# A hybrid decoder layer in seven-product matmuls: the first step on each set of w_out's operands, from eight block products to seven

## The chip, the cores and the metric

The kernel runs on one core of a Trainium2 chip. The metric is the device time of one execution in microseconds (us). An execution has a span, from the first to the last instruction in the profile, and a time, which is a little longer. PE is TensorE, PEld its weight loads, DVE is VectorE, ACT is ScalarE, POOL is GpSimd, SP is SyncE, which here only issues DMAs.

## The reference

A layer over 2048 positions of width 1024: one RMS norm, one input projection to 6144 columns, two token mixers, a norm per head with a gate, one output projection, a residual and a last norm. All is float32.

```python
xn = rms_norm(h, ln_g)
proj = jnp.einsum('bsd,de->bse', xn, w_in)
b_gate, c_gate, x_conv, g_conv, x_lru, g_lru = jnp.split(proj, splits, axis=-1)
y_conv = headwise_rms_norm(short_conv_mixer(b_gate, c_gate, x_conv, conv_w), N_CONV_HEADS, conv_out_g) * silu(g_conv)
y_lru  = headwise_rms_norm(rg_lru_mixer(x_lru, ...), N_LRU_HEADS, lru_out_g) * silu(g_lru)
h = h + jnp.einsum('bse,ed->bsd', concatenate([y_conv, y_lru]), w_out)
return rms_norm(h, final_g)
```

## The kernel before, in words

**Products.** Both projections are cut into 64 steps. A step is a 2x2 block matrix product (stationary blocks S, moving blocks T), done as a Strassen-Winograd scheme with seven products of sums of blocks, numbered 0 to 6. Each operand is split into a high and a low part (`th` and `tl`, or the two halves of a tile `s`), and a product of 128 columns by 512 over four blocks j is 12 matmuls: for each j `s_hi*th`, `s_hi*tl`, `s_lo*th`. Products 0, 1 and 2 add up in one PSUM bank that ACT copies out on the way (`q`, `u`, `rr`); DVE adds the banks and these copies (`combine`).

**Steps.** Steps 0 to 23 and 24 to 47 (kinds l, a, b) are the input projection on the first and second half of the positions; steps 48 to 55 and 56 to 63 (kind o) are the output projection, on the two halves of w_out's rows. Each of these four runs has its own set of 28 pairs of T tiles (7 operands by 4 blocks j). There is room for one set, so a new set replaces the old one tile by tile, at the change from one run to the next. For w_out the set changes between steps 47 and 48 (the first change here) and between steps 55 and 56 (the second).

**Order.** The order on every engine is the order in which the code is written (`manual_schedule`). The loop over steps `n` runs through slots `s`; a slot issues the small work that is due (`tick`), the work of a change of set (`change.slot(q)`), loads or casts for the next step's S tiles (`prep`), and then one product on PE. An ordinary step has seven slots; slot 1 holds product 6 of the step before (`pend`). The last step on an old set has an eighth slot for its own product 6.

**The first step on a set, before.** It does not use the seven sums. It forms the four blocks of the result as eight plain block products in eight slots, on four raw S tiles (`BLOCKS`) and four raw T operands 0, 4, 5 and 7. The step after it runs `late`: its products come in the order `AFTER` = 0, 4, 5, 1, 3, 2, and product 6 in the step after that.

**A change of set, before.** `Change.of_w(q)` is called with q = 0 to 7 in the last old step, 8 to 15 in the first new step and 16 to 21 in the late one. In q = 1 to 8 it cuts 16 raw tiles of w_out (`cut`: an ACT cast for the high part, a DVE subtraction for the low one). `place` loads a sum made earlier from `td` in DRAM into the tile that becomes its low part, at q = 6, 7, 9, 15 for operands 3, 1, 2, 6; these are cut from q = 11 on, operand 6 last, at q = 18 and 19.

**Work prepared ahead.** `jobs` runs in the background of steps 30 to 46. It prepares the S tiles of steps 48, 49, 56 and 57 and stores them to `so`: four raw tiles for the first step on each set (even m), seven for the second (odd m). It also makes the w_out sums and stores them to `td`. The S tiles of later o steps are made from loads of y (`raw<-yd`) and its norms (`zr<-rsd`): DVE multiplies them (`raw<-raw,zr`) and then forms the sums. In steps 56 on, DVE also adds the partial result of the earlier half, loaded from `od` (`ob<-ob,xr`).

**Queues.** All loads are issued by SP in order. DVE and ACT also work in order: an instruction that waits for a load holds up all behind it.

Of the kernel before, what the change touches and what calls it, by code (L numbers as in the profile page):

```python
# [15 lines left out]
ALU = mybir.AluOpType  # L16
# [22 lines left out]
def hymba_kernel(ctx: ExitStack, tc: tile.TileContext, x, xt, w_in, par, lamc, w_gate, w_out, final_g, out):  # L39
# [30 lines left out]
    def aux(name):  # L70
        return small.tile([P, C], F32, tag="aux", bufs=4, name=name)
# [195 lines left out]
    def opens(n):  # L267
        return n > 0 and set_of(n) != set_of(n - 1)


    def load_z(h, m, zr, wait):
        r = [piece("raw") for _ in range(4)]
        fs = []
# [68 lines left out]
    def jobs():  # L342
        tjobs = [(t, j) for t in (2, 3) for j in range(NB)]
        for ph, m in ((0, 0), (0, 1), (1, 2), (1, 3)):
# [5 lines left out]
            for f in fs[2:]:  # L350
                f()
            yield
            if m % 2:
                x_ = aux("s3")
                tt(x_, a11, a21, ALU.subtract)
                tt(a21, a21, a22, ALU.add)
            b = {}

            def blocks():
# [21 lines left out]
            blocks()  # L381
            prev = None
            nothing = lambda: None
            if m % 2:
                items = [(0, a11, lambda: tt(a11, a21, a11, ALU.subtract)), (3, x_, nothing), (2, a21, nothing),
                         (1, a11, nothing), (4, a12, lambda: tt(a12, a12, a11, ALU.subtract)),
                         (6, a22, nothing), (5, a12, nothing)]
            else:
                items = [(n, v, nothing) for n, v in enumerate((a12, a22, a11, a21))]
            for n, (i, v, after) in enumerate(items):  # L390
                if prev:
                    prev()
# [29 lines left out]
    class Change:  # L422
        def __init__(self, t, dst):
            self.t, self.dst, self.r = t, dst, {}
            old = dict(home)
            for i, was in ((5, 0), (4, 1), (0, 3), (7, 2), (3, 4), (1, 5), (2, 6), (6, 2)):
                home[i] = old[was]
            self.order = [(i, j) for i in (5, 4, 0, 7) for j in range(NB)]
            self.loaded = self.split = 0

        def slot(self, q):
# [49 lines left out]
        def of_w(self, q):  # L481
            if q == -3:
                self.load(4)
            if 1 <= q <= 8:
                todo = self.order[self.split:2 * q]
                self.cut(todo)
                self.split += len(todo)
                self.load(min(16, self.split + 6))
            if q in (6, 7, 9, 15):
                self.place((3, 1, 2, 6)[(6, 7, 9, 15).index(q)])  # L490
            self.cut({11: ((3, 0), (3, 1)), 12: ((3, 2), (3, 3)), 13: ((1, 0), (1, 1)), 14: ((1, 2), (1, 3)),
                      15: ((2, 0), (2, 1)), 16: ((2, 2), (2, 3)), 18: ((6, 0), (6, 1)),
                      19: ((6, 2), (6, 3))}.get(q, ()))

        def place(self, i):
            for j in range(NB):
# [3 lines left out]

        def load(self, n):
            for i, j in self.order[self.loaded:n]:
                b = {0: 0, 7: 1, 4: 2, 5: 3}[i]
                self.r[i, j] = piece("traw")
                nc.sync.dma_start(self.r[i, j], w_blocks(self.t, j)[b])
            self.loaded = max(n, self.loaded)
# [503 lines left out]
    def load_next(n, d=2):  # L1010
        if n < N:
            Sn[n] = {}
            kind, h, k = steps[n]
            src = None
            if kind == "o":
                src = so[h, k] if (h, k) in made else None
            elif h == 1 and (k > 0 or kind == "l"):
                src = sd[3 * k + "lab".index(kind)]
            order = {}
            if opens(n):  # L1020
                order = dict(order=BLOCKS, at_=range(4) if kind == "o" else BLOCKS)
            elif opens(n - 1):
                order = dict(order=AFTER, at_=AFTER)
            plan[n] = s_loads(src, Sn[n], **order) if src is not None else s_plan(n, load_s(n, d), Sn[n])

# [6 lines left out]
    with tc.manual_schedule(engines={ENG.PE, ENG.Activation, ENG.DVE, ENG.Pool, ENG.SP}):  # L1032
# [177 lines left out]
        for n in range(PLAIN, N):  # L1210
# [2 lines left out]
            last = n + 1 == N  # L1213
            new = not last and set_of(n + 1) != set_of(n)
            soon = n + 2 < N and set_of(n + 2) != set_of(n + 1)
            put = lru(h, k, 2) if opens(n) and kind == "l" else consumer[kind](h, k)
            if n == 3 * KT + 6:
                work_on[0] = jobs()
            if opens(n):
                cc = {}  # L1220
                for s, (which, i, t) in enumerate(((12, 1, 5), (22, 3, 5), (11, 1, 4), (21, 3, 4),
                                                   (11, 0, 0), (12, 0, 7), (22, 2, 7), (21, 2, 0))):
# [11 lines left out]
                    if s == 4:  # L1234
                        load_next(n + 2, 4)
                continue
            late = opens(n - 1)
            bk = {}
            slots = (0, 6) + ORDER[1:] if not late else AFTER
            for s in range(6 if late else 8 if new or last else 7):  # L1240
# [7 lines left out]
                    change.slot(s - 8)  # L1248
                if new:
                    change.slot(s)  # L1250
                if late:
                    change.slot(16 + s)
                    if s == 0:
                        prep(n, 7)
                elif n > 0 and opens(n - 2):
                    if s == 0:
                        prep(n, 5)
                        prep(n, 6)
                    elif s == 2:
                        prep(n, 7)  # L1260
                elif s == 0:
                    prep(n, 6)
                elif s == 2:
                    prep(n, 7)
                if new and s > 0:
                    if s in (1, 3, 4, 5):
                        prep(n + 1, (1, 3, 4, 5).index(s) + 1)
                    elif s > 5:
                        prep(n + 2, s - 5)
                elif s > 0:  # L1270
                    prep(n + 1, s - 1)
# [87 lines left out]
```

## Time and profile before

| | us |
|---|---|
| median of 3 runs | 1329.51 (1328.81 to 1329.94) |
| the profiled execution, its own time | 1328.63 |
| its span | 1326.9 |
| PE busy | 1295.0 (98%) |
| DVE busy | 1041.1 (78%) |
| ACT busy | 748.7 (56%) |
| granted clock, mean | 0.996 |

PE has 5688 matmuls, 5448 of them on line 993 (`mm`). In a row of the timeline the first number is the start in us from the span's start, the second the duration; `x2` merges two equal instructions; in brackets at the end stand the idle time of the engine before it and what ended that. A duration of a matmul includes its way through the array, so matmuls overlap, and their pitch is shorter than their duration.

### The profile page before, as it was taken

The page shows a single profiled execution, that of the slowest core. Times are in us where ns is not written, and L with a number is a line of the kernel's source. Part 1 is how long each engine was busy: PE and PEld are TensorE (multiplying, and loading weights), DVE is VectorE, ACT ScalarE, POOL GpSimd, SP SyncE. Part 2 cuts the span into 40 slices and gives each one's busy share as a digit, 9 for nine tenths or more (in the row PEclk, how much of TensorE's full clock was granted, in tenths as well). Part 3 has the DMA queues.
Part 4 walks back from the last instruction along what each step waited for, and adds up shares of the span by engine and source line. Part 5 has one row for each costly group of instructions (what it writes and reads, how often), then busy time and mean ns, then how long its engine had stood idle before and what let it go on. Part 6 is the DMA issues. An engine that isn't in the chain of part 4 may idle for free.

```text
span 1326.9 us, 16682 instructions
## 1 busy us (share of the span) xinstructions
PE 1295.0 (98%) x5688; PEld 1059.2 (80%) x5688; DVE 1041.1 (78%) x1251; ACT 748.7 (56%) x1141; POOL 249.6 (19%) x190
## 2 busy tenths in 40 slices
PE   7989999999999999899999999999999999999997
PEld 6867778787878787778888888888888888887886
DVE  7888898999989897979566675667549777659886
ACT  7585758566675657466544545354457433445453
POOL 3204333344334340102010101102011000000000
PEclk9999999999999999999999999999999999999999
DMA  7147777888989888452689999999789987697754
GB/s 291 32 151 246 283 282 249 301 322 284 340 287 325 293 295 302 163 164 97 218 319 298 331 345 337 343 341 366 246 271 323 279 253 250 220 404 286 233 180 160
DMA packets 157958, 355.29 MB, mean 268 GB/s; under 512 B 16944, under 2 KB 51760, under 8 KB 157872
## 3 DMA queue, kind: packets, MB, share of 16 engines
q1 hardware_dynamic: 153264, 338.17, 74.1%
q0 software_dynamic: 4320, 15.73, 3.0%
q8 instruction: 45, 0.74, 0.2%
q14 instruction: 41, 0.34, 0.1%
q10 hardware_dynamic: 288, 0.32, 0.1%
HBM read 217.11 MB, written 137.04 MB: 267 GB/s over the span
## 4 chain that ended last, share of the span: by engine, by line
PE 57%; DVE 21%; DMA 8%; ACT 7%; issue 6%; SPq 1%; POOL 0%; DVEq 0%; ACTq 0%
PE bank L993 54%; DVE s L163 4%; DVE tl L163 2%; DMA s<-so 2%; DVE st L163 2%; PE gate L730 2%; DVE u L704 2%; DVE r L764 2%; ACT i L737 1%; ACT r L737 1%; DVE traw L163 1%; DVE sums L635 1%; DMA raw<-in_w_in_dram 1%; DVE raw L163 1%; DVE u L163 1%
## 5 line engine op out<-in xcount | busy, mean ns | idle before, releaser
L993 PE MATMUL bank<-th,s 128*128 128x512 f32 x3632 | 1132.8, 391 | 13.3 <-ACT q L1293 6.4
L993 PEld LDWEIGHTS bank<-th,s 128*128 128x128 f32 x3632 | 683.1, 188 | 163.1 <-ACT q L1293 7.6
L993 PE MATMUL bank<-tl,s 128*128 128x512 f32 x1816 | 708.6, 390 | 2.3 <-DVE tl L163 2.1
L993 PEld LDWEIGHTS bank<-tl,s 128*128 128x128 f32 x1816 | 341.8, 188 | 75.1 <-DVE tl L163 3.6
L163 POOL TENSOR_TENSOR s<-raw,s 128x512 fp32r<-128x512 f32 x62 | 111.3, 1808 | 248.7 <-ACT s L200 207.9
L200 ACT CAST s<-raw 128x512 fp32r<-128x512 f32 x140 | 85.3, 617 | 78.1 <-PE bank L993 44.4
L163 POOL TENSOR_TENSOR gb<-gb,sg 128x1024 f32<-128x1024 f32 x16 | 43.4, 2712 | 331.0 <-ACT sg L663 292.5
L163 DVE TENSOR_TENSOR s<-raw,s 128x512 fp32r<-128x512 f32 (+1 forms) x125 | 89.4, 738 | 8.6 <-ACT s L1052 4.4
L163 DVE TENSOR_TENSOR s<-s,s 128x512 fp32r<-128x512 f32 x105 | 87.8, 836 | 1.9 <-ACT s L200 1.9
L163 DVE TENSOR_TENSOR tl<-traw,th 128x512 fp32r<-128x512 f32 x85 | 61.0, 750 | 25.1 <-ACT th L438 16.9
L200 ACT CAST s<-s 128x512 fp32r<-128x512 f32 x105 | 64.8, 617 | 13.8 <-DVE s L163 13.8
L704 DVE SCALAR_TENSOR_TENSOR u<-xl,pt,u 128x1024 f32<-128x1024 f32 x48 | 64.4, 1342 | 6.5 <-ACT u L700 5.9
L1293 ACT COPY q<-bank 128x512 f32<-128x512 f32 x58 | 33.9, 584 | 54.4 <-PE bank L993 44.9
L814 DVE SCALAR_TENSOR_TENSOR t<-p,pt,t 128x1024 f32<-128x1024 f32 x32 | 46.5, 1454 | 15.9 <-ACT t L811 15.1
L737 ACT ACTIVATE r<-gate,pt 64x512 f32<-64x512 f32 x64 | 43.7, 683 | 17.3 <-PE gate L730 16.5
L163 DVE TENSOR_TENSOR st<-u,st 64x1024 fp32r<-64x1024 f32 x32 | 49.5, 1547 | 1.2 <-ACT st L715 0.3
L1296 ACT COPY rr<-bank 128x512 f32<-128x512 f32 x31 | 18.1, 584 | 55.5 <-PE bank L993 55.5
L1296 ACT COPY u<-bank 128x512 f32<-128x512 f32 x27 | 15.8, 585 | 54.1 <-PE bank L993 53.9
L163 DVE TENSOR_TENSOR raw<-raw 128x512 f32<-128x512 f32 x41 | 44.9, 1096 | 0.2
L163 DVE TENSOR_TENSOR traw<-traw 128x512 f32<-128x512 f32 x60 | 41.9, 699 | 3.6 <-DMA traw<-in_w_out_dram 2.1
L737 ACT ACTIVATE i<-gate,pt 64x512 f32<-64x512 f32 x64 | 43.7, 683 | 1.1
L163 POOL TENSOR_TENSOR gl<-gl,sg 128x1024 f32<-128x1024 f32 x16 | 40.1, 2508 | 19.0 <-ACT sg L663 19.0
(168 smaller groups left out, 1262.3 us busy)
## 6 DMA issues: line engine op xcount, KB each, us to landing
sd<-s SPq DMA_DIRECT2D x151, 512.0 KB
s<-sd SPq DMA_DIRECT2D x151, 512.0 KB
raw<-in_w_in_dram SPq DMA_DIRECT2D x104, 256.0 KB
raw<-yd SPq DMA_DIRECT2D x64, 256.0 KB
traw<-in_w_out_dram SPq DMA_DIRECT2D x64, 256.0 KB
so<-so SPq DMA_DIRECT2D x22, 512.0 KB
s<-so SPq DMA_DIRECT2D x22, 512.0 KB
yd<-gl SPq DMA_DIRECT2D x32, 256.0 KB
```

Source lines behind the costliest of these rows:

```text
L163: (eng or nc.vector).tensor_tensor(out=out, in0=a, in1=b, op=op)
L200: nc.scalar.copy(dst[i][0], val(i))
L635: nc.vector.tensor_reduce(out=sums[0][:, kt * R:(kt + 1) * R].rearrange("p (q b) -> p q b", q=4), in_=y.rearrange("p (b q a) -> p q b a", ...
L704: nc.vector.scalar_tensor_tensor(out=v["u"], in0=o1[:, 1 + j:1 + j + N2], scalar=lw[j], in1=v["u"], op0=ALU.mult, op1=ALU.add)
L730: nc.tensor.matmul(ps[j], v["gw"][n][:, j, :], v["st"][j][:, sl], start=(n == 0), stop=(n == 1))
L737: nc.scalar.activation(out=g_[hi, sl], in_=v["ps"][j][src], func=AF.Sigmoid, bias=pt[src, bias + k:bias + k + 1])
L764: nc.vector.tensor_tensor_scan(out=r, data0=r, data1=v["u"], initial=init, op0=ALU.mult, op1=ALU.add)
L814: nc.vector.scalar_tensor_tensor(out=tcur["t"], in0=p[:, 2 + j:2 + j + N2], scalar=cw[j], in1=tcur["t"], op0=ALU.mult, op1=ALU.add)
L993: nc.tensor.matmul(bank, a[:, js], b, start=start and n == 0, stop=stop and n == 2, skip_group_check=more)
L1293: nc.scalar.copy(q1, bk["A"])
L1296: nc.scalar.copy(u2, bk["A"])
```

## The change

The first step on each of w_out's two sets takes the same seven products as the other steps, in the order `AFTER`, with product 6 in the following step; the step after it is an ordinary one. Step 24, of kind l, keeps its eight block products (`whole`). W_out's change of set uses slots q = 0 to 14 in place of 0 to 19: three raw operands (12 cuts) at q = 1 to 6, four placed ones, loaded at q = 5 to 8 and cut at q = 8 to 14. `jobs` prepares seven S tiles for steps 48 and 56 too. PE has 24 matmuls less (5664).

```diff
+    def whole(n):
+        return opens(n) and steps[n][0] == "l"
+
+    def late_at(n):
+        return n > 0 and (whole(n - 1) or (opens(n) and not whole(n)))
...
-            if m % 2:
-                items = [(0, a11, lambda: tt(a11, a21, a11, ALU.subtract)), (3, x_, nothing), (2, a21, nothing),
-                         (1, a11, nothing), (4, a12, lambda: tt(a12, a12, a11, ALU.subtract)),
-                         (6, a22, nothing), (5, a12, nothing)]
-            else:
-                items = [(n, v, nothing) for n, v in enumerate((a12, a22, a11, a21))]
+            items = [(0, a11, lambda: tt(a11, a21, a11, ALU.subtract)), (3, x_, nothing), (2, a21, nothing),
+                     (1, a11, nothing), (4, a12, lambda: tt(a12, a12, a11, ALU.subtract)),
+                     (6, a22, nothing), (5, a12, nothing)]
...
-            if 1 <= q <= 8:
+            if 1 <= q <= 6:
                 todo = self.order[self.split:2 * q]
                 self.cut(todo)
                 self.split += len(todo)
-                self.load(min(16, self.split + 6))
-            if q in (6, 7, 9, 15):
-                self.place((3, 1, 2, 6)[(6, 7, 9, 15).index(q)])
-            self.cut({11: ((3, 0), (3, 1)), 12: ((3, 2), (3, 3)), 13: ((1, 0), (1, 1)), 14: ((1, 2), (1, 3)),
-                      15: ((2, 0), (2, 1)), 16: ((2, 2), (2, 3)), 18: ((6, 0), (6, 1)),
-                      19: ((6, 2), (6, 3))}.get(q, ()))
+                self.load(min(12, self.split + 6))
+            if 5 <= q <= 8:
+                self.place((1, 3, 2, 6)[q - 5])
+            self.cut({8: ((1, 0), (1, 1)), 9: ((1, 2), (1, 3)), 10: ((3, 0), (3, 1)), 11: ((3, 2), (3, 3), (2, 0)),
+                      12: ((2, 1), (2, 2), (2, 3)), 13: ((6, 0), (6, 1)), 14: ((6, 2), (6, 3))}.get(q, ()))
...
-            if opens(n):
-                order = dict(order=BLOCKS, at_=range(4) if kind == "o" else BLOCKS)
-            elif opens(n - 1):
+            if whole(n):
+                order = dict(order=BLOCKS, at_=BLOCKS)
+            elif late_at(n):
                 order = dict(order=AFTER, at_=AFTER)
...
-            late = opens(n - 1)
+            late = late_at(n)
...
+                if opens(n - 1) and not late and s == 0:
+                    change.slot(14)
                 if late:
-                    change.slot(16 + s)
+                    change.slot(16 + s if kind != "o" else 8 + s)
```

DVE, at the first change, from the end of step 48 into step 49 (`tl<-tl,th`: the low part of a placed T tile; `sums`, `rt`: norms of the heads; `raw<-raw,zr`: y times its norm for step 50). Before:

```order
L163 TENSOR_TENSOR tl<-tl,th 128x512 x6
L635 TENSOR_REDUCE sums<-t 128x32
L163 TENSOR_TENSOR rt<-sums,rt 128x512
L163 TENSOR_TENSOR tl<-tl,th 128x512 x2
L163 TENSOR_TENSOR raw<-raw,zr 128x512 x2
L163 TENSOR_TENSOR tl<-tl,th 128x512 x2
L163 TENSOR_TENSOR raw<-raw,zr 128x512 x2
```

Now:

```order
L637 TENSOR_REDUCE sums<-r 128x32
L163 TENSOR_TENSOR tl<-tl,th 128x512 x5
L163 TENSOR_TENSOR ob<-bank,rr 128x512 x2
L163 TENSOR_TENSOR raw<-raw,zr 128x512 x2
L163 TENSOR_TENSOR tl<-tl,th 128x512 x2
L637 TENSOR_REDUCE sums<-t 128x32
L163 TENSOR_TENSOR rt<-sums,rt 128x512
L163 TENSOR_TENSOR raw<-raw,zr 128x512 x2
```

The two cuts between the pairs of `raw<-raw,zr` were the last ones of operand 2 and are now the last ones of operand 6; those of operand 6 came four rows later before.

DVE, at the second change, from step 55 into step 57 (`xr<-xr,ob`, `ob<-ob,xr`: adding partial results; `ob<-bank,...`: a product's bank into the result). Before:

```order
L163 TENSOR_TENSOR tl<-tl,th 128x512 x6
L163 TENSOR_TENSOR ob<-ob,xr 128x1024
L163 TENSOR_TENSOR tl<-tl,th 128x512 x4
L163 TENSOR_TENSOR raw<-raw,zr 128x512 x2
L163 TENSOR_TENSOR ob<-ob,xr 128x1024
L163 TENSOR_TENSOR tl<-tl,th 128x512 x2
L163 TENSOR_TENSOR raw<-raw,zr 128x512 x2
```

Now:

```order
L163 TENSOR_TENSOR tl<-tl,th 128x512 x4
L163 TENSOR_TENSOR ob<-bank,q_9994 128x512
L163 TENSOR_TENSOR tl<-tl,th 128x512 x10
L163 TENSOR_TENSOR ob<-bank,rr 128x512 x2
L163 TENSOR_TENSOR raw<-raw,zr 128x512 x2
L163 TENSOR_TENSOR ob<-ob,xr 128x1024
L163 TENSOR_TENSOR tl<-tl,th 128x512 x2
```

Fourteen cuts of placed operands now stand ahead of the first `raw<-raw,zr`; the last two, of operand 6, stand behind it and behind the first `ob<-ob,xr`.

SP, at the second change, up to the load for that first `ob<-ob,xr` (`s<-so_124`, `s<-so_125`: S tiles of steps 56 and 57; `fg`: the last gain; `tl<-td_130` to `td_133`: a placed operand; `xr<-od_138`). Before:

```order
L868 DMA fg<-in_final_g_dram 128x1024
L226 DMA s<-so_125 128x1024
L499 DMA tl<-td_130 128x512
L499 DMA tl<-td_131 128x512
L499 DMA tl<-td_132 128x512
L499 DMA tl<-td_133 128x512
L226 DMA s<-so_125 128x1024
L873 DMA xr<-od_138 128x1024
L226 DMA s<-so_125 128x1024
L294 DMA raw<-yd_86 128x512 x2
```

Now:

```order
L870 DMA fg<-in_final_g_dram 128x1024
L501 DMA tl<-td_130 128x512
L501 DMA tl<-td_131 128x512
L501 DMA tl<-td_132 128x512
L501 DMA tl<-td_133 128x512
L226 DMA s<-so_124 128x1024
L226 DMA s<-so_125 128x1024 x2
L300 DMA raw<-yd_86 128x512 x2
L290 DMA zr<-rsd_89 128x1024
L300 DMA raw<-yd_86 128x512 x2
L290 DMA zr<-rsd_89 128x1024
L875 DMA xr<-od_138 128x1024
```

Ahead of `xr<-od_138` now stand all four loads of y with their norms, and the fourth placed operand (before, the fourth came behind both `xr` loads).

More of the change, by code (lines that the diff above doesn't have):

```diff
@@ L352, in jobs @@
             yield
-            if m % 2:
-                x_ = aux("s3")
-                tt(x_, a11, a21, ALU.subtract)
-                tt(a21, a21, a22, ALU.add)
+            x_ = aux("s3")
+            tt(x_, a11, a21, ALU.subtract)
+            tt(a21, a21, a22, ALU.add)
             b = {}
@@ L383, in jobs @@
             nothing = lambda: None
-            if m % 2:
-                items = [(0, a11, lambda: tt(a11, a21, a11, ALU.subtract)), (3, x_, nothing), (2, a21, nothing),
-                         (1, a11, nothing), (4, a12, lambda: tt(a12, a12, a11, ALU.subtract)),
-                         (6, a22, nothing), (5, a12, nothing)]
-            else:
-                items = [(n, v, nothing) for n, v in enumerate((a12, a22, a11, a21))]
+            items = [(0, a11, lambda: tt(a11, a21, a11, ALU.subtract)), (3, x_, nothing), (2, a21, nothing),
+                     (1, a11, nothing), (4, a12, lambda: tt(a12, a12, a11, ALU.subtract)),
+                     (6, a22, nothing), (5, a12, nothing)]
             for n, (i, v, after) in enumerate(items):
@@ L425, in __init__ @@
             old = dict(home)
-            for i, was in ((5, 0), (4, 1), (0, 3), (7, 2), (3, 4), (1, 5), (2, 6), (6, 2)):
+            for i, was in (((5, 0), (4, 1), (0, 3), (7, 2), (3, 4), (1, 5), (2, 6), (6, 2)) if t == 1 else
+                           ((0, 0), (4, 1), (5, 3), (1, 2), (3, 4), (2, 5), (6, 6))):
                 home[i] = old[was]
-            self.order = [(i, j) for i in (5, 4, 0, 7) for j in range(NB)]
+            self.order = [(i, j) for i in (0, 4, 5) for j in range(NB)]
             self.loaded = self.split = 0
@@ L502, in load @@
             for i, j in self.order[self.loaded:n]:
-                b = {0: 0, 7: 1, 4: 2, 5: 3}[i]
+                b = {0: 0, 4: 2, 5: 3}[i]
                 self.r[i, j] = piece("traw")
@@ L1215, in hymba_kernel @@
             soon = n + 2 < N and set_of(n + 2) != set_of(n + 1)
-            put = lru(h, k, 2) if opens(n) and kind == "l" else consumer[kind](h, k)
+            put = lru(h, k, 2) if whole(n) else consumer[kind](h, k)
             if n == 3 * KT + 6:
                 work_on[0] = jobs()
-            if opens(n):
+            if whole(n):
                 cc = {}
@@ L1250, in hymba_kernel @@
                     change.slot(s)
+                if opens(n - 1) and not late and s == 0:
+                    change.slot(14)
                 if late:
-                    change.slot(16 + s)
+                    change.slot(16 + s if kind != "o" else 8 + s)
                     if s == 0:
                         prep(n, 7)
-                elif n > 0 and opens(n - 2):
+                elif late_at(n - 1):
                     if s == 0:
@@ L1264, in hymba_kernel @@
                     prep(n, 7)
-                if new and s > 0:
+                if new and s > 0 and whole(n + 1):
                     if s in (1, 3, 4, 5):
```

## The prediction, made before the changed kernel ran

> **What bounds the kernel now.** I read the page's busy times first, then the chain that ended last, PE's waits, and tables by stretches of 10 us around the two places where w_out's set changes.
>
> ```profile
> span 1326.9 us, 16682 instructions
> PE 1295.0 (98%) x5688; PEld 1059.2 (80%) x5688; DVE 1041.1 (78%) x1251; ACT 748.7 (56%) x1141; POOL 249.6 (19%) x190
> PE 57%; DVE 21%; DMA 8%; ACT 7%; issue 6%; SPq 1%; POOL 0%; DVEq 0%; ACTq 0%
> ```
>
> PE is the bound of nearly the whole span, so matmuls taken away there are worth their pitch, as long as nothing else is late. Whether something is shows in the stretches (columns: PE, PEld, DVE, ACT and POOL busy, granted clock, DMA share, GB/s):
>
> ```profile
> 1010.00:1020.00 10.00, 10.00 (x46) 8.29 (x45) 8.37 (x7) 4.26 (x7) 3.28 (x1) 1.00 1.06 381
> 1020.00:1030.00 10.00, 10.00 (x46) 8.29 (x45) 9.13 (x13) 7.69 (x14) 1.27 (x2) 1.00 1.01 283
> ...
> 1150.00:1160.00 10.00, 10.00 (x46) 8.29 (x45) 6.44 (x11) 4.50 (x10) 0.00 (x0) 1.00 1.01 361
> 1160.00:1170.00 10.00, 10.00 (x46) 8.29 (x45) 7.96 (x11) 4.74 (x9) 1.07 (x2) 1.00 1.04 408
> 1170.00:1180.00 10.00, 10.00 (x46) 8.29 (x45) 1.43 (x3) 3.10 (x6) 0.00 (x0) 1.00 1.04 402
> 1180.00:1190.00 10.00, 10.00 (x46) 8.29 (x45) 4.93 (x7) 5.22 (x11) 0.00 (x0) 1.00 1.04 403
> 1190.00:1200.00 10.00, 9.14 (x41) 7.25 (x40) 9.15 (x14) 5.15 (x10) 0.53 (x1) 1.00 1.04 398
> 1200.00:1210.00 10.00, 8.92 (x40) 7.04 (x39) 9.96 (x17) 5.16 (x10) 0.53 (x1) 1.00 0.82 300
> ```
>
> At both changes PE runs without a gap while the DMA engines are full (share 1.01 and more) for tens of us; DVE is nearly full too at the first. At the second, 400 GB/s seems to be all that the transfers get. PE is covered there only by how early things were asked for, and the change asks for them later against PE.
>
> **What the change takes away.** The eight block products of an old first step show in ACT's copies of their banks, one per product from the fifth on. First row: the sixth product of step 48; the others: the sixth to eighth of step 56.
>
> ```profile
> 1022.20 0.59 ACT L793 COPY ob<-bank 128x512 f32<-128x512 f32 x1 [0.82 <-PE bank L993]
> ...
> 1178.52 0.59 ACT L793 COPY ob<-bank 128x512 f32<-128x512 f32 x1 [1.04 <-PE bank L993]
> 1181.24 0.59 ACT L793 COPY ob<-bank 128x512 f32<-128x512 f32 x1 [1.09 <-PE bank L993]
> 1183.96 0.59 ACT L793 COPY ob<-bank 128x512 f32<-128x512 f32 x1 [1.09 <-PE bank L993]
> ```
>
> They are 2.72 us apart: one product, 12 matmuls, 0.227 us each. Two products fewer are worth 5.44 us. A copy starts some 0.2 us behind its product, so step 48 goes from 1005.7 to 1027.4, and step 56 from 1162.0 to 1183.8. With six products in these steps, the next ones would begin at 1022.0 and 1178.3, and product 6 of the first step (in slot 1 of the next) at 1024.7 and 1181.0. PE's waits near here, which may go or stay:
>
> ```profile
> PE bank L993 <- ACT rr L1296: 0.5, 1, 0.5
> ...
> 1198.38 0.50 PE L993 MATMUL bank<-th,s 128*128 128x512 f32 x1 [0.86 <-ACT rr L1296]
> 1205.20 0.50 PE L993 MATMUL bank<-th,s 128*128 128x512 f32 x1 [1.08 <-DVE ob L163]
> ```
>
> The first is the only wait of PE from 990 to 1060. Each comes of ACT or DVE being behind in the step after the first; if PE is held up before, they have caught up, so I count all three as gone: -0.45 and -1.94.
>
> **First change, DVE's queue.** Product 6 now needs its low parts a step earlier. The cuts of its blocks 2 and 3 stand behind the first pair of `raw<-raw,zr`, and that pair waits for a load:
>
> ```profile
> 1011.07 3.28 POOL L163 TENSOR_TENSOR gb<-gb,sg 128x1024 f32<-128x1024 f32 x1 [35.67 <-ACT sg L663]
> ...
> 1008.01 1.29 DVE L163 TENSOR_TENSOR tl<-traw,th 128x512 fp32r<-128x512 f32 x2
> 1009.22 0.68 DVE L163 TENSOR_TENSOR gb<-bank,rr 128x512 f32<-128x512 f32 x1
> 1009.82 2.34 DVE L764 TENSOR_TENSOR_SCAN r<-r,hl,u 128x1024 f32<-128x1024 f32 x1
> 1012.08 3.42 DVE L163 TENSOR_TENSOR tl<-traw,th 128x512 fp32r<-128x512 f32 x2
> 1015.42 1.27 DVE L645 SCALAR_TENSOR_TENSOR gl<-r,pt,gl 128x1024 f32<-128x1024 f32 x1
> ...
> 1020.74 1.25 DVE L635 TRANSPOSE_TENSOR_REDUCE sums<-r 128x32 f32<-128x1024 f32 x1
> 1021.90 3.68 DVE L163 TENSOR_TENSOR tl<-tl,th 128x512 fp32r<-128x512 f32 x6
> ...
> 1029.51 1.29 DVE L163 TENSOR_TENSOR raw<-raw,zr 128x512 f32<-128x512 f32 x2 [0.22 <-DMA zr<-rsd]
> 1030.73 1.29 DVE L163 TENSOR_TENSOR tl<-tl,th 128x512 fp32r<-128x512 f32 x2
> ```
>
> Six cuts take 3.68, a pitch of 0.60; the pair at 1012.08 took 2.13 more than two others (1.29), while POOL's multiplication `gb<-gb,sg` (first row) ran beside it. The scan now has the two cuts of 1008.01 less ahead of it, 1.2, so it starts at 1008.6. From there DVE has the scan (2.3), 14 cuts (8.4), POOL's hold (2.1), two `f1` of 1.2, one reduction (1.2) and three bank additions of 0.7 (2.1): it comes to the `raw` pair at 1027.1. The last cut of operand 2, for the sixth product, is done two cuts and two bank additions earlier (2.5), at 1024.6; PE has two matmuls left then and ends step 48 at 1025.1, 3.1 late. Then the pair waits for `zr`. On SP the bytes from the twelfth raw tile of w_out, the last in both orders, up to that `zr` are the same: four raw tiles fewer (1.05 MB), one placed operand more (1.05 MB), eight S tiles in both. The queue is full, so I keep 1029.5. The cut of block 2 is done at 1029.51 + 1.22 + 0.69 = 1031.4, and five matmuls later (1.1) the next product begins at 1032.5, where a PE without stalls would begin it at 1027.4: 5.1 us lost (it contains the 3.1). Net: -2.72 + 5.1 - 0.45 = **+1.9**. Low end, if `zr` is there when DVE comes: 3.1 lost, -0.1. High end, with a further us from S tiles of step 49, asked for behind the y loads: +2.9.
>
> **Second change, SP's queue.** DVE has time here, but the same two cuts stand behind `raw<-raw,zr` and `ob<-ob,xr`:
>
> ```profile
> 1175.12 0.32 SPq L873 DMA_DIRECT2D xr<-od  x1
> 1182.96 0.32 SPq L873 DMA_DIRECT2D xr<-od  x1
> ...
> 1182.99 1.23 DVE L163 TENSOR_TENSOR ob<-ob,xr 128x1024 f32<-128x1024 f32 x1 [4.69 <-DMA xr<-od]
> 1184.13 2.49 DVE L163 TENSOR_TENSOR tl<-tl,th 128x512 fp32r<-128x512 f32 x4
> 1186.94 1.29 DVE L163 TENSOR_TENSOR raw<-raw,zr 128x512 f32<-128x512 f32 x2 [0.32 <-DMA zr<-rsd]
> 1190.78 1.22 DVE L163 TENSOR_TENSOR ob<-ob,xr 128x1024 f32<-128x1024 f32 x1 [2.54 <-DMA xr<-od]
> ```
>
> The placed operands 1, 3 and 2, asked for from slots 5 to 7 of the old step on (1154), wait on SP for the old product that reads their tiles, with S tiles queued behind them; at 7.8 us from issue to use they are there by 1174, and PE needs the last of them at 1177. Not so operand 6. DVE waited for both `xr`, and each landed 7.8 us behind its issue. Ahead of the first `xr` SP now has 1.05 MB for the fourth placed operand, one S tile (0.52) and the four y loads with two norms (2.10) more, and four raw tiles (1.05) less: +2.62 MB. At the 402 GB/s of these stretches it lands 6.5 us later, at 1189.5. The S tile that step 57 opens with has the bytes ahead that the first `xr` had, without the last half MB: 1.3 us before 1183.0, so PE waits at 1178.3 until 1181.7, does product 0 and seven matmuls of product 6 (to 1186.0), and waits again for the cut at 1189.5 + 1.14 + 0.69 = 1191.3. The next product begins at 1192.4 instead of 1183.8: 8.7 lost. Net: -2.72 + 8.7 - 1.94 = **+4.0**. Low end: if the queue, not full before 1160 (the stretch 1150 to 1160 moved 361), takes half of the added bytes for nothing, 5.4 lost, +0.7. High end, at 361 GB/s: 7.3 for 6.5, +4.8.
>
> **The clock.** A gap of 5.3 us at PE has a price of its own:
>
> ```profile
> 97.21 0.79 PE L993 MATMUL bank<-th,s 128*128 128x512 f32 x1 [3.06 <-ACT q L1293]
> ...
> 97.00:100.20 3.20, 2.99 (x7) 2.41 (x8) 3.17 (x4) 3.17 (x5) 0.00 (x0) 0.50 0.72 258
> ```
>
> Behind a gap of 3.06 the granted clock was 0.50, and PE did 7 matmuls in 3.2 us instead of 14: 1.6 us. Behind the gaps of 1.08 and less above, it stayed at 1.00. I take **+1.5**; ends 0 and +1.7.
> The Trainium skill, TensorE: Matmul & The Clock Gate, section "Part 1: The HAM clock gate", says that the clock halves only after a whole idle window of some 3.4 us, and that the window runs freely. By that rule a gap of 5.3 may or may not hold a whole window, and the sum without a drop is 1.5 lower; the gap of 3.06 here was shorter than such a window and the clock fell all the same.
>
> **The rest.** Per set, four cuts fall away on ACT and DVE (in the sum above) and an ACT copy becomes DVE additions (in it too). The two jobs each make three more S tiles: three casts, three subtractions and four sums of a tile, three stores of 0.52 MB, in steps 30 to 43, and every later part of the jobs moves by some slots. PE there has one gap in 400 us:
>
> ```profile
> L993 PE MATMUL bank<-th,s 128*128 128x512 f32 x1135 | 352.3, 389 | 0.6 <-DMA s<-sd 0.6
> ```
>
> DVE's and ACT's part is covered by PE's products; if that cover fails, a bank copy is late next. I take 0; ends -0.6 (this gap goes) and +1 (another like it, since the y loads now follow other stores).
>
> **Sum.** 1.9 + 4.0 + 1.5 = +7.4 on the profiled execution's 1328.63: 1336.0. The median of the runs is 0.9 above that execution, well inside the range, so I leave it at 1336.0. Ends: +0.0 - 0.1 + 0.7 - 0.6, so about 1328.6, and 2.9 + 4.8 + 1.7 + 1 = +10.4, 1339.0; I take 1328.5 to 1340.
>
> **Rivals.**
> *The loads are in time, and it is faster.* PE's 5.44 and the old waits are then saved: 1328.63 - 5.44 - 2.39 = 1320.8; with the first change as forecast, 1325.4. It decides at the first `xr`: landed before 1180.8 (1182.6, when PE needs the cut, less 1.8 of DVE), 8.7 earlier than I expect. For it: SP is ahead of PE by four raw tiles at 1154. Against: 2.6 MB more at 400 GB/s.
> *Short waits.* Both changes at their low ends and no drop of the clock: +0.6 to +3, 1329 to 1332, no change that can be told. For it: DMA had 361 GB/s before 1160 and may have had room.
> *The clock stays full*, by the skill's window or because the wait is split in two: 1334.5. Slower all the same.
> *More stalls.* The S tiles of step 57, asked for behind the two `xr`, land late too: over 1340. Against: they land 1 to 4 us behind the first `xr`, and PE is 8.7 later.
> That the change doesn't remove the products can't be: PE's order has 24 matmuls less.
>
> **Chances.** Forecast with the clock's drop 0.43, without it 0.20, more stalls 0.05: slower 0.68. Short waits 0.20. In time 0.12. By over 0.2% is 2.7 us, about what a measurement here can tell from no change: faster 0.12, same 0.20, slower 0.68.
>
> **What would show it.** PE's waits should have a new one of some 5 us near 1186, with a cut `tl` by name, DVE behind `xr<-od`; one of 2 to 3 near 1024 to 1030 before a `tl`, DVE behind `zr<-rsd`; a granted clock of 0.50 for 3 us behind the first. The prediction is wrong if the first `xr` lands before 1185 or PE has no gap before a `tl` in these places.

## The result, and the profile after

| | before | after |
|---|---|---|
| median of the runs (us) | 1329.94 (5 runs, 1328.81 to 1330.55) | 1343.55 (5 runs, 1340.8 to 1345.6) |
| the profiled execution, its own time | 1328.63 | 1345.6 |
| its span | 1326.9 | 1343.8 |

After over before is 1.0105, with a 95% interval of 1.0093 to 1.0116: 13.6 us slower by the medians, 16.9 between the two profiled executions (that of the changed kernel is the slowest of its five runs). The direction was as forecast, the size was not: 1336.0 was forecast, 1340 was the upper end.

From the page of the changed kernel, its span, its busy times and the chain that ended last:

```profile
span 1343.8 us, 16674 instructions
PE 1295.1 (96%) x5664; PEld 1057.3 (79%) x5664; DVE 1049.0 (78%) x1263; ACT 748.5 (56%) x1139; POOL 248.7 (19%) x190
PE 53%; DVE 20%; DMA 13%; issue 6%; ACT 5%; SPq 2%; POOL 0%; DVEq 0%; ACTq 0%; POOLq 0%
```

PE has 24 matmuls less and is as long busy as before, mostly since some of them ran at half the clock. In the chain PE went from 57% to 53%, DMA from 8% to 13%. What PE waited for in the whole span (us in total, times, longest):

```profile
PE bank L995 <- DVE tl L163: 9.6, 8, 3.7
...
PE bank L995 <- DMA s<-sd: 5.8, 1, 5.8
PE bank L995 <- DMA s<-so: 4.6, 3, 3.5
```

Before, the row with `tl` had 2.1 us, that with `s<-sd` 0.6, and there was no wait for `s<-so`. The 5.8 us of `s<-sd` are one wait, and it stands far from both changes of set, as the three long gaps on PE's timeline show:

```profile
752.04 0.80 PE L995 MATMUL bank<-th,s 128*128 128x512 f32 x1 [5.82 <-DMA s<-sd]
...
1193.33 0.80 PE L995 MATMUL bank<-th,s 128*128 128x512 f32 x1 [3.47 <-DMA s<-so]
...
1203.09 0.57 PE L995 MATMUL bank<-tl,s 128*128 128x512 f32 x1 [3.66 <-DVE tl L163]
```

The first is the start of step 35, in the stretch where `jobs` prepares work; the others are products 0 and 6 in step 57. The same columns by stretches of 10 us as in the prediction:

```profile
740.00:750.00 10.00, 6.22 (x28) 4.80 (x26) 6.55 (x9) 4.87 (x7) 1.43 (x1) 0.97 1.07 243
750.00:760.00 10.00, 7.96 (x26) 6.42 (x27) 1.96 (x4) 1.10 (x2) 0.00 (x0) 0.69 1.03 404
1020.00:1030.00 10.00, 9.01 (x38) 6.45 (x36) 10.00 (x12) 7.38 (x14) 2.48 (x1) 1.00 1.05 391
1030.00:1040.00 10.00, 7.04 (x30) 5.48 (x31) 7.57 (x13) 3.16 (x5) 0.73 (x1) 1.00 1.06 216
1190.00:1200.00 10.00, 6.10 (x19) 4.59 (x19) 3.23 (x6) 2.13 (x5) 0.00 (x0) 0.83 1.04 405
1200.00:1210.00 10.00, 6.91 (x23) 5.54 (x24) 8.65 (x13) 3.17 (x7) 0.00 (x0) 0.83 1.03 405
```

PE has holes at step 35, at the first change (1020 to 1040) and at the second (1190 to 1210), each with the DMA engines full, and the granted clock falls behind the first and the last.

Where the time went can be told for the two profiled executions, because PE's order of matmuls is known: take the start of a step in each trace, after minus before. The difference grows by 7.9 us from step 34 to step 48 (the jobs), by 2.8 from 48 to 50 (the first change), by 6.1 from 56 to 59 (the second), and by 0.2 elsewhere: 16.9 in sum. These three numbers are used for every kernel below.

**The jobs.** In both kernels the y loads of the second job take SP some 9 us. Before, SP issues four td stores, and then these loads at slot 4 of step 33; four S tiles follow, for the steps being computed:

```profile
715.04 1.80 SPq L378 DMA_DIRECT2D td<-traw  x4
...
719.48 0.67 SPq L294 DMA_DIRECT2D raw<-yd  x1
...
726.76 1.69 SPq L287 DMA_DIRECT2D zr<-rsd  x2
728.55 2.83 SPq L226 DMA_DIRECT2D s<-sd  x4
```

After, the first job has seven tiles, so the same things come five slots later, at slots 1 and 2 of step 34:

```profile
726.66 0.43 SPq L678 DMA_DIRECT2D bd<-in_w_gate_dram  x1
732.09 2.18 SPq L383 DMA_DIRECT2D td<-traw  x4
...
735.52 0.82 SPq L300 DMA_DIRECT2D raw<-yd  x1
...
742.53 1.65 SPq L293 DMA_DIRECT2D zr<-rsd  x2
744.36 5.07 SPq L226 DMA_DIRECT2D s<-sd  x7
```

SP stands from 727.1 to 732.1 before the td stores, whose sums DVE has not yet made, and only then issues the y loads. Seven S tiles have piled up behind them. One is for product 0 of step 35, which is asked for five slots ahead of its use, where the others have six. It is used at 752.04. The stop there and the slow clock behind it, less the old wait of 0.6, make 7.1 of the 7.9; nearly all of the rest is one stop of 0.4 in step 43, where PE waited for a copy of ACT, and no other kernel's profile has that stop.

**First change.** DVE from the scan to the last cuts of operand 6:

```profile
1016.69 2.34 DVE L766 TENSOR_TENSOR_SCAN r<-r,hl,u 128x1024 f32<-128x1024 f32 x1
1018.95 1.27 DVE L163 TENSOR_TENSOR tl<-tl,th 128x512 fp32r<-128x512 f32 x2
1020.14 3.43 DVE L647 SCALAR_TENSOR_TENSOR gl<-r,pt,gl 128x1024 f32<-128x1024 f32 x1
...
1030.66 3.05 DVE L163 TENSOR_TENSOR tl<-tl,th 128x512 fp32r<-128x512 f32 x5
1034.15 1.29 DVE L163 TENSOR_TENSOR ob<-bank,rr 128x512 f32<-128x512 f32 x2 [0.44 <-ACT rr L1303]
1037.44 1.29 DVE L163 TENSOR_TENSOR raw<-raw,zr 128x512 f32<-128x512 f32 x2 [1.99 <-DMA zr<-rsd]
1038.65 1.29 DVE L163 TENSOR_TENSOR tl<-tl,th 128x512 fp32r<-128x512 f32 x2
```

This is the forecast order: DVE behind, POOL's hold (2.2 us, now on `gl`), then the pair that waits for `zr` ahead of the cuts.

**Second change.** The first `xr` on SP's timeline:

```profile
1193.35 0.32 SPq L875 DMA_DIRECT2D xr<-od  x1
```

And on DVE's, what waits for it and for `zr` of the same queue:

```profile
1197.30 1.29 DVE L163 TENSOR_TENSOR raw<-raw,zr 128x512 f32<-128x512 f32 x2 [5.36 <-DMA zr<-rsd]
...
1201.21 1.23 DVE L163 TENSOR_TENSOR ob<-ob,xr 128x1024 f32<-128x1024 f32 x1 [2.62 <-DMA xr<-od]
1202.35 1.29 DVE L163 TENSOR_TENSOR tl<-tl,th 128x512 fp32r<-128x512 f32 x2
```

It landed 7.9 us behind its issue, and the cuts came after it.

### The profile page after: what moved, and what is told of

It reads as the page before. It is cut to its first block, busy times and chain, and to the rows that moved or that the text cites. A ratio compares the mean times of both kernels' runs of the same rounds, so it can differ in the third digit from the quotient of the medians.

```text
span 1343.8 us, 16674 instructions
## 1 busy us (share of the span) xinstructions
PE 1295.1 (96%) x5664; PEld 1057.3 (79%) x5664; DVE 1049.0 (78%) x1263; ACT 748.5 (56%) x1139; POOL 248.7 (19%) x190
## 4 chain that ended last, share of the span: by engine, by line
PE 53%; DVE 20%; DMA 13%; issue 6%; ACT 5%; SPq 2%; POOL 0%; DVEq 0%; ACTq 0%; POOLq 0%
PE bank L995 51%; DVE s L163 5%; DMA s<-so 2%; DVE u L706 2%; DVE tl L163 2%; DMA tl<-td 2%; DVE st L163 2%; PE gate L732 2%; DVE traw L163 1%; DVE sums L637 1%; DMA raw<-in_w_in_dram 1%; DMA xcol<-in_xt_dram 1%; DMA s<-sd 1%; DVE r L766 1%; DMA sd<-s 1%
## 5 line engine op out<-in xcount | busy, mean ns | idle before, releaser
L163 DVE TENSOR_TENSOR tl<-traw,th 128x512 fp32r<-128x512 f32 x77 | 53.7, 729 | 25.2 <-ACT th L441 13.4
L739 ACT ACTIVATE r<-gate,pt 64x512 f32<-64x512 f32 x64 | 43.8, 684 | 16.9 <-PE gate L732 16.1
L163 DVE TENSOR_TENSOR raw<-raw,zr 128x512 f32<-128x512 f32 x64 | 41.3, 686 | 12.4 <-DMA zr<-rsd 12.3
L163 DVE TENSOR_TENSOR raw<-raw 128x512 f32<-128x512 f32 x47 | 49.1, 1044 | 0.4
```

The lines of the kernel that those rows point to most:

```text
L163: (eng or nc.vector).tensor_tensor(out=out, in0=a, in1=b, op=op)
L739: nc.scalar.activation(out=g_[hi, sl], in_=v["ps"][j][src], func=AF.Sigmoid, bias=pt[src, bias + k:bias + k + 1])
```

## The experiments

Theory A: the three costs are separate and each is one of order: the y loads of the jobs ahead of an S tile that has little slack; DVE's backlog and the cuts behind `zr`; the bytes ahead of `xr` on SP. Theory B: the three more S tiles per job (three stores of 0.52 MB each) cost time wherever they stand. The other rivals are given with each run. Time is the median, the ratio is to the kernel before on the same chip with its 95% interval. The kernels ran on several chips, so two kernels are best compared by their ratios. The last three columns come from one profiled execution of each: how much the difference of PE's step starts to those of before grows over these steps (us).

| kernel | time | ratio | 34 to 48 | 48 to 50 | 56 to 59 |
|---|---|---|---|---|---|
| after | 1343.55 | 1.0105 [1.0093, 1.0116] | 7.9 | 2.8 | 6.1 |
| jobs_shift | 1336.81 | 1.0058 [1.0042, 1.0074] | -0.9 | 2.9 | 6.2 |
| jobs_alone | 1337.35 | 1.0065 [1.0047, 1.0083] | 7.4 | 0.1 | -0.2 |
| second_only | 1334.36 | 1.0044 [1.0027, 1.0062] | -0.7 | 0.2 | 6.4 |
| first_only | 1339.75 | 1.0081 [1.0066, 1.0096] | 8.2 | 1.2 | 0.3 |
| cut_ahead | 1339.5 | 1.0068 [1.0053, 1.0083] | 7.4 | 2.1 | 0.8 |
| bytes_early | 1342.4 | 1.0087 [1.007, 1.0104] | 7.7 | 1.3 | 3.4 |
| clock_fill | 1342.31 | 1.0091 [1.0077, 1.0105] | 4.6 | 2.2 | 6.9 |
| best | 1328.07 | 0.998 [0.9969, 0.9991] | -0.9 | 1.6 | -3.8 |
| td_pool | 1339.9 | 1.0082 [1.0065, 1.0098] | 3.4 | 2.1 | 7.2 |
| dve_relief | 1328.22 | 0.9995 [0.9986, 1.0004] | -0.9 | 4.2 | -3.7 |
| best2 | 1327.7 | 0.9983 [0.9975, 0.9992] | -0.9 | -0.7 | 0.7 |
| best3 | 1324.17 | 0.9963 [0.9949, 0.9977] | -0.9 | -0.3 | -3.9 |

### The jobs: jobs_shift, jobs_alone, td_pool

**jobs_shift**, the changed kernel with a pause behind the first job:

```diff
-            yield from (None,) * 2
+            yield from (None,) * (4 if (ph, m) == (0, 0) else 2)
```

> The changed kernel with two more slots of pause behind the first job, so that the y loads of the second job are issued in step 34, slot 4, as before the change, and no longer in slot 2 behind the td stores; the later jobs move by one slot at most. Theory A (the place of these loads on SP: the S tile for product 0 of step 35 stands behind them): PE's 5.8 us gap at the start of step 35 is under 1 us, the clock there stays at 1.00, and the time falls by about 7, to 1335 to 1338. Theory B (the three more S tiles per job, 1.57 MB of stores each, cost time wherever they stand): 1342 to 1345, with the gap somewhere else in steps 34 to 37.

PE has no wait at all in 690 to 800, and the time is within theory A's range: 7.7 above the kernel before instead of 13.6. SP still stands before the td stores, but three S tiles now go ahead of the y loads:

```profile
733.26 1.78 SPq L383 DMA_DIRECT2D td<-traw  x4
...
737.74 1.44 SPq L226 DMA_DIRECT2D s<-sd  x3
739.22 0.42 SPq L300 DMA_DIRECT2D raw<-yd  x1
```

The same instructions and bytes, two slots later: theory B falls.

**jobs_alone**, the kernel before with seven tiles in the even jobs, three of them used by nothing:

```diff
-                items = [(n, v, nothing) for n, v in enumerate((a12, a22, a11, a21))]
+                items = [(0, a12, nothing), (1, a22, nothing), (2, a11, nothing),
+                         (3, a21, lambda: tt(a21, a21, a22, ALU.add)),
+                         (4, x_, lambda: tt(a11, a21, a11, ALU.subtract)),
+                         (5, a21, lambda: tt(a12, a12, a11, ALU.subtract)), (6, a12, nothing)]
```

> The kernel before, where the first and the third job also make seven S tiles (three of them, and four sums, are not used by anything), with the slots of the changed kernel; nothing is changed where the sets change. Theory A: 8 us slower than before, some 1337.5, with a gap of 5 to 6 us at the start of step 35 and the clock at 0.50 behind it. Rival: the jobs cost so much only together with the changed steps 48 and 56: 1329 to 1331.

8.2 slower, with one long wait, in step 35:

```profile
PE bank L996 <- DMA s<-sd: 6.4, 1, 6.4
```

So the largest cost of the change is there without any change at steps 48 and 56.

**td_pool**, the changed kernel with the td stores on POOL's queue:

```diff
-                    at(1, lambda: [nc.sync.dma_start(to[n], v) for n, v in enumerate((b22, b11, b12, b21))])
+                    at(1, lambda: [nc.gpsimd.dma_start(to[n], v) for n, v in enumerate((b22, b11, b12, b21))])
```

> The changed kernel with the stores of the w_out sums to td issued by POOL instead of SP; the y loads keep their place in step 34, slot 2. Theory A1 (half of the jobs' cost is SP standing 5.3 us before the td stores until DVE has the sums, with the y loads and the S tiles behind them): the S tile of step 35 comes 5 us earlier, PE's gap there falls from 5.8 to about 1, the clock stays, and the time falls by 6 to 7, to 1336 to 1338. Theory A2 (the 9 us of y loads ahead of that S tile are enough by themselves): a gap of 4 to 5.8 us stays, 1341 to 1344.

Neither: the gap at the start of step 35 fell to 2.4, as PE's timeline shows.

```profile
748.60 0.50 PE L995 MATMUL bank<-th,s 128*128 128x512 f32 x1 [2.37 <-DMA s<-sd]
```

The granted clock (third number from the end in the table by stretches) fell all the same, for 3.4 us instead of 6.8.

```profile
750.00:753.00 3.00, 3.00 (x9) 2.35 (x8) 0.00 (x0) 0.00 (x0) 0.00 (x0) 0.50 1.03 410
```

Step 35 lost 4.3 instead of 8.1. SP's stand before the td stores is worth 3.8 of it; the y loads ahead of the S tile, the rest. How much of that rest comes of the y loads' new slot, and how much of the tile being asked for a slot later than the others, was not taken apart.

### One change at a time: second_only, first_only

In **second_only** step 48 keeps its eight block products and its old change of set, in **first_only** step 56:

```diff
     def whole(n):
-        return opens(n) and steps[n][0] == "l"
+        return opens(n) and (steps[n][0] == "l" or set_of(n) in OLD)
+
+    OLD = (2,)
```

(`OLD = (3,)` in first_only; with it go the raw tiles of that job, and the old operands, places and slots in that `Change`)

> Only step 56 takes seven products; step 48 keeps its eight block products, so the first job makes four tiles and the y loads of the second job stay in step 33, slot 4. Theory A: +6 from the second change, +0.7 from the last job's place: 1335 to 1337. Theory B (tiles cost time wherever they stand, half of 8 for one job): 1338 to 1341.

> Only step 48 takes seven products; step 56 keeps its eight. Theory A: +7.3 from the first job's shift of the y loads, +2.8 from the first change: 1338 to 1341, with the gap at the start of step 35. Theory B (half of 8 for one job, +2.8): 1335 to 1337.

Both are clearly outside theory B, and the costs stand where theory A has them. Second_only, 5.2 slower, is 0.6 below theory A's range: all its cost stands at steps 56 to 58, and the 0.7 expected for the last job's place did not come. First_only is 10.6 slower, of which 8.2 stand in the jobs. The first change itself came out between 1.2 and 2.9 in six executions that have it as changed (after, jobs_shift, first_only, bytes_early, clock_fill, td_pool; median 2.2).

### The cuts, the bytes, the clock: cut_ahead, bytes_early, clock_fill

**cut_ahead**, the changed kernel with the last cuts of operand 6 ahead of the slot's due work:

```diff
+                if opens(n - 1) and not late and s == 0:
+                    change.slot(14)
                 tick()
...
-                if opens(n - 1) and not late and s == 0:
-                    change.slot(14)
```

> The changed kernel with the cuts of operand 6, blocks 2 and 3, written ahead of the slot's other work in steps 49 and 57, so that on DVE they stand before the pair of multiplications by zr (and, in step 57, before the addition of xr). Theory A (these cuts are late for their place in DVE's queue alone): PE's waits of 1.6 us in step 49 and of 3.7 us in step 57 go, and with the latter one of the two clock drops (1.7 us): 7.0 less, 1335.5 to 1338. The 3.5 us wait for the S tile of step 57 stays. Rival (their own loads from td are late too, or the banks' additions are the next to be late): 2 to 4 less, 1339.5 to 1341.5, with a wait of 1 to 3 us left in step 57 or 58.

The time, 1339.5, is at the edge of the rival's range and not in theory A's. At the second change alone it is as theory A has it, 5.3 less: of PE's waits in 1140 to 1240 the one for the cuts is gone.

```profile
PE bank L995 <- DMA s<-so: 3.9, 2, 3.5
```

At the first change it is not told apart from the spread of the others (2.1 against 1.2 to 2.9): the wait for the cuts went, and one for an S tile of step 49 came instead, here of 2.0.

```profile
PE bank L995 <- DVE tl L163: 2.4, 3, 1.6
PE bank L995 <- DMA s<-so: 2.0, 1, 2.0
```

**bytes_early**, the changed kernel with `fg` loaded in step 52, and the xr loads of step 55 four slots earlier:

```diff
-        if ph == 1 and m == 2:
+        if ph == 0 and m == 4:
             fg[0] = wt("t", "fg")
...
-            at(5, lambda: load(0))
-            at(6, lambda: load(1))
+            at(1 if (ph, m) == (0, 7) else 5, lambda: load(0))
+            at(2 if (ph, m) == (0, 7) else 6, lambda: load(1))
```

> The changed kernel with 1.57 MB taken out of SP's crowded stretch before step 57: the broadcast load of fg moves from step 56 to step 52, the two xr loads of step 55 from its slots 4 and 5 to 0 and 1. Theory A (the S tile that opens step 57 is late by the bytes ahead of it: 1.57 MB at 404 GB/s is 3.9 us): the 3.5 us wait at the start of step 57 goes with its clock drop (1.7): 5.2 less, 1337 to 1339.5; the wait before the cuts of operand 6 stays at 3 to 4 us, since PE and xr are earlier by the same. Rival (SP's issue, held up by buffers, sets it): within 1.5 of the changed kernel, 1342 to 1345.

The wait for the S tile at the start of step 57 is gone, so the bytes were its cause. But only 2.7 were won at this change, and the time, 1342.4, is in the rival's range, though not for the rival's reason: the wait for the cuts grew.

```profile
1198.71 0.80 PE L995 MATMUL bank<-tl,s 128*128 128x512 f32 x1 [5.16 <-DVE tl L163]
```

PE came there 5.4 earlier (a wait of 3.47, its restart, and the slow clock behind it), the landing of `xr` that fixes the cut only the 3.9 of its bytes: 3.66 + 1.5 = 5.16. My expectation had both move alike.

**clock_fill**, the changed kernel with transposes in PE's waits, whose results are not used:

```diff
+                if (n, s) == (35, 0):
+                    for _ in range(40):
+                        nc.tensor.transpose(bk[b][:, 0:P], ident, ident)
+                if (n, s) == (57, 0):
+                    spun[0] = None
+                    spin(24)
...
                         for j in range(NB):
+                            if (n, j) == (57, 2):
+                                spin(24)
                             mm(B, S6, T, 6, j, alone and j == 0, j == NB - 1, not alone)
```

> The changed kernel with PE kept at work in its three long waits by 128x128 transposes whose results are not used: 40 ahead of product 0 of step 35, 24 ahead of product 0 of step 57, 24 between blocks 1 and 2 of product 6 in step 57. The waits themselves stay. Theory A (each drop of the granted clock to 0.50 costs half its length: 3.4, 1.7 and 1.7 us): 6.8 less, 1335.5 to 1338, with the clock at 1.00 through steps 35 and 57. Rival (PE would only reach its next wait sooner, or transposes don't count for the clock): 1341 to 1346.

The time is in the rival's range, and in steps 56 to 58 for its first reason. In step 35 the clock stayed at 1.00 and 2.5 us were won, not 3.4: of the 6.8 us at half clock PE had worked only in the last 4.2 (752.0 to 756.2), which cost some 2; the S tile also came 0.5 earlier against PE's steps. At step 57 nothing was won.

```profile
1186.20 2.78 PE L531 MATMUL spin<-ident 128*128 128x128 f32 x24
1189.86 0.50 PE L995 MATMUL bank<-th,s 128*128 128x512 f32 x1 [0.87 <-DMA s<-so]
...
1194.10 2.78 PE L531 MATMUL spin<-ident 128*128 128x128 f32 x24
1200.53 0.78 PE L995 MATMUL bank<-tl,s 128*128 128x512 f32 x1 [3.41 <-DVE tl L163]
```

The first drop was avoided, but PE then only stood longer before the cuts, whose time `xr` sets; and the rest of that wait, 3.41, still brought a drop. Td_pool shows the same without any transposes: there the clock stayed at 1.00 behind the first wait of step 57 (3.47, as in the changed kernel), and the second was 5.39 instead of 3.66.

### Taking the costs away: best, dve_relief, best2, best3

**best** is the changed kernel with the edits of jobs_shift, cut_ahead and bytes_early.

> The changed kernel with three edits together: two more slots of pause behind the first job, the cuts of operand 6 ahead in steps 49 and 57, and fg and the xr loads of step 55 earlier. Theory A: the added costs go one by one, -7.3 for the jobs, -1.6 at the first change, -7 to -10 at the second: 1324.5 to 1328, that is 1 to 4 below the kernel before, of the 5.4 that two products are worth; what is left is DVE's backlog at the first change (2 to 3 us). Rival (the second change is bound by its transfers as a whole): a wait of 3 us or more in step 57, 1329 to 1333.

1328.07, at the upper end of theory A's range and 0.2% below the kernel before. The second change is now worth 3.8, the jobs 0.9 (the old wait of 0.6 in step 34 is gone); the first still costs 1.6.

**dve_relief** takes 2.2 us of DVE's time out of the first change:

```diff
-        at(d0 + 3, lambda: head_sums(h, kt, y))
+        at(d0 + (4 if h and kt == 2 * KT - 1 else 3), lambda: head_sums(h, kt, y))
...
-        at(4 + late, lambda: tt(g, g, sg[0], ALU.mult, nc.gpsimd))
+        at(4 + late, lambda: tt(g, g, sg[0], ALU.mult, eng or nc.gpsimd))
...
-                silu(g)
+                silu(g, 0, nc.vector if h and k == KT - 1 else None)
```

> The kernel with the three edits, and 2.2 us taken out of DVE's queue ahead of the last cuts of operand 2 at the first change: the multiplication gb by sg of step 47 runs on DVE (1.2 us) instead of POOL, beside which a DVE instruction took 2.2 longer, and the reduction of r (1.25 us) comes one slot later. Theory A (what is left of the first change's cost is DVE's backlog): PE's waits for cuts in step 48, 1.6 and 0.6 us, go, and the time falls by 1.5 to 2.2, to about 1326. Rival (step 49 waits for an S tile from so in any case): that wait of 1.5 us grows by what was won, and the gain is under 0.7, 1327.4 to 1328.5.

The time is in the rival's range, and by the profile the first change now costs 4.2, where it cost 1.6 in best. Step 48 was 2.2 shorter, but the S tile of step 49 came when it came: PE's wait for it grew from 1.5 to 3.7, and the clock was at 0.50 for 6.8 us behind it.

```profile
1034.26 0.80 PE L995 MATMUL bank<-th,s 128*128 128x512 f32 x1 [3.70 <-DMA s<-so]
```

**best2** also moves the y loads behind those S tiles:

```diff
-                if s == 3:
-                    load_next(n + 2, 3 if late else 4)
+                if s == (5 if late and kind == "o" else 3):
+                    load_next(n + 2, 1 if late and kind == "o" else 3 if late else 4)
```

> The same with the y loads of steps 50 and 58 issued two slots later (slot 5 of steps 48 and 56), behind the S tiles of slots 4 and 5. Theory A (S tiles and cuts are all that PE waits for there): the S wait in step 49 goes too, 3 to 3.7 below the kernel with three edits, 1324 to 1325.5. Rival (zr then comes later, and DVE's additions of the banks stand behind raw by zr): a new wait of PE for a bank in step 49, 50, 57 or 58, and 1326 to 1329.

The time, 1327.7, is in the rival's range; by the profile both theories hold, one at each change. The first is now 0.7 better than before. At the second `zr` comes later, DVE's `ob<-ob,xr` stands behind it, ACT's square of `ob` behind that, and the copy that frees PE's bank behind ACT's square:

```profile
1191.93 0.50 PE L995 MATMUL bank<-th,s 128*128 128x512 f32 x1 [2.89 <-ACT rr L1300]
```

**best3** moves the y loads of step 50 alone:

```diff
-                if s == (5 if late and kind == "o" else 3):
-                    load_next(n + 2, 1 if late and kind == "o" else 3 if late else 4)
+                if s == (5 if n == 48 else 3):
+                    load_next(n + 2, 1 if n == 48 else 3 if late else 4)
```

> The kernel with the three edits and the relief of DVE, where the y loads of step 50 alone come two slots later (slot 5 of step 48); those of step 58 stay in slot 3 of step 56. Theory A (each change is bound by what PE waits for there, and the two do not touch each other): the first change costs as little as with both loads moved (-0.7 over steps 48 and 49 instead of +1.6), the second as little as with three edits (-3.8 over steps 56 to 58), with no wait of PE over 1.2 us in either: a span of 1321 to 1323, 4 to 6 below the profiled execution of the kernel before, and a time of 1324 to 1326. Rival (the gain at the first change is lost again before step 56): 1327 to 1328.5.

4.8 below the kernel before, as theory A has it (-0.3 instead of -0.7 at the first change). PE's waits that are left, first in 1000 to 1080, then in 1140 to 1240:

```profile
PE bank L995 <- ACT rr L1300: 1.0, 1, 1.0
PE bank L995 <- DVE tl L163: 0.7, 1, 0.7
PE bank L995 <- DMA s<-so: 0.3, 1, 0.3
...
PE bank L995 <- DMA s<-so: 0.8, 2, 0.6
```

These 4.8 are not the two products alone. In the stretches of the table the stops of the kernel before that are gone were worth 4.1 (the waits of 0.59, 0.45, 0.86 and 1.08, each with 0.28 for the restart, see below), and the stops that are left cost about as much. The same moves of loads were not tried on the kernel before, so how much they would win there by themselves is not shown.

## Why the prediction was wrong, step by step

- **The rest: the step that failed.** The jobs' change was taken as 0, at most +1, and cost 7.9. I looked for cover on DVE and ACT, where it was, and named the y loads' new place ("now follow other stores") without working out which S tiles stand behind them on SP and how much slack those have. The rows of before had it: y loads of 9 us on SP, S tiles in a heap behind them, and the wait of 0.6 that I took for the size of such an event was the mark of a place without slack. Shifted by five slots, the same loads met the one S tile with a slot less, behind td stores that wait for DVE. Jobs_alone (7.4 with nothing else changed) and jobs_shift (-0.9) show that this is all of it but the 0.7 in step 43. With it in the sum, the forecast would have been 1343.9, against 1345.6 for the profiled execution; the rest is 0.9 at the first change, 0.6 at the second and 0.2 elsewhere.
- **What the change takes away**: 2.72 per product, right. Step 48 is 2.2 shorter than before: 5.44 for two products fewer, less 3.2 for its waits.
- **First change, +1.9**: 2.8 in the profiled execution, 2.2 as the median of six. Each stop of PE costs 0.28 more than its listed idle time (below). With that, the waits of step 48 (2.37 in three stops) cost 3.2, forecast 3.1; the one for the cut behind `zr` 1.9, forecast 2.0; the old wait that goes 0.7, forecast 0.45. The S tile of step 49, 1.1, was in the upper end only. Dve_relief and cut_ahead show that it is not one more event but the floor under the other two: take those away, and it takes their place.
- **Second change, +4.0**: the mechanism as forecast, at the forecast places. The first wait was 3.47 (forecast 3.4), the second 3.66 before a cut behind `xr`, which landed 7.9 behind its issue (7.8). The second was forecast at 5.3, since the sum let PE reach it at full clock: PE began the step 0.8 later than forecast and took 1.8 longer to that point, at half clock, while the end of the wait, set by `xr`, came only 1.0 later. The old waits that go were worth 2.5 with their stops, forecast 1.94.
- **The clock, +1.5**: here it fell behind both waits. The first drop costs nothing, as clock_fill and td_pool show, since PE waits for `xr` afterwards; the second costs 1.7. With it the second change comes to 6.1, forecast 5.5. The drop that was not forecast is the one in step 35, 2.0 us.
- **By the rule weighed there**, that the clock halves only after a whole idle window of some 3.4 us (the Trainium skill, TensorE: Matmul & The Clock Gate, "Part 1: The HAM clock gate"), td_pool's gap could not have brought a drop. It was 2.37 and did. The length of the slow stretch does agree with such windows: in all profiles 3.4 or 6.8 us, nothing between, but for those that the end of the kernel cuts short.
- **The rivals**: none came. No transfer was in time at the second change, and step 58 had no stall. The time is over 1340, as under "more stalls", but not for the reason given there. One sum there is off: in time at the second change with the first as forecast makes 1325.9, not 1325.4, since the old wait of 0.45 was taken off twice.

## What to carry to other kernels

When a change makes background work longer, follow everything that it shifts through each in-order queue, and ask of the foreground loads that then stand behind it how much slack they have: here the same 9 us of loads cost 0.6 us or nothing at one slot and 8 at another. Waits that end at fixed landings do not add: taking away the first (the cuts, DVE's backlog, the slow clock) only lengthens the wait for the next transfer unless that is moved too. Here the change became worth 4.8 us only after the order of the transfers was made again around it.

## What the runs showed of the hardware

- **A stop of PE costs 0.28 us more than the idle time listed.** At full clock, with gaps of 0.45, 0.59 and 1.65, the pitch of the two matmuls around the restart was 0.84 and 0.34, 0.98 and 0.34, 2.04 and 0.34, against 0.227: together 0.28 above the gap each time.
- **The clock falls behind gaps that are shorter than its slow stretch, and not always.** A gap of 2.37 halved it for 3.4 us (td_pool), and so did one of 1.88 in first_only, at 118.6 us, though one of 3.09 at 97 us had left it there. But a gap of 3.47 in td_pool left it at 1.00, as the first row behind the gap and the stretch that follows it show:

```profile
1188.44 0.50 PE L995 MATMUL bank<-th,s 128*128 128x512 f32 x1 [3.47 <-DMA s<-so]
...
1190.00:1193.00 3.00, 3.00 (x14) 2.19 (x12) 0.59 (x1) 0.59 (x1) 0.00 (x0) 1.00 1.05 402
```

  One gap of 2.9 to 3.0, at 556 to 558 us in all 14 profiled executions, halved it in six and left it in eight. One us of the table by stretches, in the kernel before:

```profile
558.00:559.00 1.00, 1.00 (x4) 0.80 (x3) 1.00 (x2) 0.72 (x1) 0.20 (x1) 0.50 0.99 397
```

And in the changed kernel:

```profile
558.00:559.00 1.00, 1.00 (x6) 0.82 (x5) 1.00 (x2) 0.86 (x1) 0.07 (x1) 1.00 1.04 426
```

  In the changed kernel gaps of 3.47 and 3.66 brought 3.4 us at half clock, that of 5.82 brought 6.8; so did one of 5.16 in bytes_early, one of 3.70 in dve_relief and one of only 3.08 in best3, at 97 us. From 1.9 to 3.5 us, then, the length of a gap does not tell here whether the clock falls, or for how long. Only the part of the slow stretch in which PE works costs anything.
